# Two half turns moved among the matmuls of the same slice, and a pair of slices of b loaded in two parts

## The chip, the cores and the metric

One core of a Trainium2 chip. The metric is the device time of one launch in microseconds; before the change it is 117.70 us, the median of five runs between 117.55 and 117.79.

## The reference

```
m, k, n, p = 1024, 1024, 2048, 1024        # a: m x k, b: k x n, c: n x p, float32
h = np.matmul(a, b)
h = 0.5 * h * (1 + np.tanh(np.sqrt(2 / np.pi) * (h + 0.044715 * h ** 3)))
return np.matmul(h, c).astype(np.float32)
```

Two matrix products with a gelu between them.

## The kernel before

**Stages.** The first product is made with h transposed: TensorE holds 128 columns of b as weights and streams 512 rows of a, so that 128 x 512 results of h land in one PSUM bank, and ScalarE's gelu writes them to `hT` in bf16. The first 512 columns of b are done with plain bf16 matmuls (`mm1`, line 111). Columns 512 to 1023 (`zero`), columns 1024 to 2047 (`one`) and the whole second product with c (`two`) go through `seven`, a scheme of seven block products in place of eight, with sums and differences of blocks made on VectorE (line 163) and the products on line 205. The change touches the first stage alone.

**Slices and pieces.** The contraction of 1024 is cut into eight slices k of 128. A load of a brings a *piece*: `abq[:, q, h]`, the 512 rows of half h (h = 0 upper, h = 1 lower) by 256 columns, that is slices 2q and 2q + 1. A load of b brings one slice or a pair, 512 columns wide. All but the upper piece 0 of a and the first pair of slices of b are loaded by GpSimd, with a cast from float32 to bf16 on the way, in the order in which they are issued (lines 85 to 101). The first two come through SyncE and are cast on VectorE and ScalarE.

**Turns.** a has to be transposed. `turn(h, q, bank, ab)` does a piece in two halves n = 0, 1, one for each slice: four 128 x 128 transposes on TensorE (line 138) into half n of a PSUM tile, then one copy on VectorE (line 139) into `aT[:, h, 2q + n]`. It is a generator; each `next(tn)` issues one half. From the upper turn of piece 1 on, all turns but the last use bank 7; banks 0 to 3 hold the sums of the upper half and 4 to 6 those of three tiles of the lower half. The fourth lower tile takes bank 7 when the turns there are over, and the last turn takes bank 0 when the gelu has read it.

**Order.** The schedule is written out by hand (`manual_schedule`): each engine runs its instructions in the order of the program. `block(h, tiles, ks)` issues one matmul for each tile and slice. In the loop over q = 1, 2 (lines 244 to 256), k = 2q, four matmuls of the upper half on slice k are followed by the first half of the lower turn of piece q, four on slice k + 1 by its second half; then `zero.t1(4, q)`, one subtraction of 128 x 512 on VectorE, three matmuls of the lower half on slice k, the first half of the upper turn of piece q + 1, three on slice k + 1, and its second half. The last lower turn (lines 262 to 268) lies among matmuls of the fourth lower tile, then come slices 6 and 7 of the lower half (line 274).

Of the kernel before, what the change touches and what calls it, by code (L numbers as in the profile page):

```python
# [19 lines left out]
def kernel(ctx, tc, a, b, c, out):  # L20
    nc = tc.nc
# [3 lines left out]
    H = 512  # L25
# [4 lines left out]
    bv = b.rearrange("(kt p) n -> p kt n", p=128)  # L30
# [9 lines left out]
    def slot(tag, shape, dt, name):  # L40
        return big.tile(shape, dt, name=name, tag=tag)

    def bank(i, shape=(128, H), dt=F32, name="ps"):
        return pp.tile(list(shape), dt, name=name, tag=f"bank{i}", padded_shape=None)
# [14 lines left out]
    b1 = slot("b1", [128, KT, 1024], BF16, "b1")  # L59
# [8 lines left out]
    def a_part(h, q):  # L68
        return av[:, 4 * h:4 * h + 4, ds(q * 256, 256)]

    def b_part(q):
        return bv[:, 2 * q:2 * q + 2, 0:H]
# [6 lines left out]
    def cast_load_a(h, q):  # L79
        nc.gpsimd.dma_start(out=abq[:, q, h], in_=a_part(h, q))  # L80

    def cast_load_b(q):
        nc.gpsimd.dma_start(out=b1[:, 2 * q:2 * q + 2, 0:H], in_=b_part(q))

    cast_load_a(1, 0)
    cast_load_a(0, 1)
    nc.gpsimd.dma_start(out=b1[:, 2, 0:H], in_=bv[:, 2, 0:H])
    cast_load_a(1, 1)
    nc.gpsimd.dma_start(out=b1[:, 3, 0:H], in_=bv[:, 3, 0:H])
    for q in range(2, 4):  # L90
        cast_load_a(0, q)
        cast_load_b(q)
        cast_load_a(1, q)
    for k in range(0, KT, 4):
        nc.gpsimd.dma_start(out=b1[:, k:k + 4, H:], in_=bv[:, k:k + 4, ds(H, H)])
    for n in range(2):
        for k in range(0, KT, 4):
            nc.gpsimd.dma_start(out=b2[:, k:k + 4, ts(n, H)],
                                in_=bv[:, k:k + 4, ds(1024 + n * H, H)])
# [9 lines left out]
    def mm1(p, t, h, ks):  # L109
        for k in ks:  # L110
            nc.tensor.matmul(p, b1[:, k, ts(t, 128)], aT[:, h, k],  # L111
                             start=(k == 0), stop=(k == KT - 1))
# [4 lines left out]
    ps = {(0, t): bank(t) for t in range(4)}  # L117
# [7 lines left out]
    def cast_a(eng):  # L125

        ab = pieces("ab", 2, [128, 4, 256], BF16, "ab")
        copy(eng, ab, sta[:, 0])
        return ab

    def turn(h, q, i, ab):

        banks = i if isinstance(i, tuple) else (i,)
        pts = [bank(x, (128, 2, H), BF16, "pt") for x in banks]
        for n in range(2):
            pt = pts[n % len(pts)]
            for m in range(4):
                nc.tensor.transpose(pt[:, n, ts(m, 128)], ab[:, m, ts(n, 128)], ident)  # L138
            nc.vector.tensor_copy(aT[:, h, 2 * q + n], pt[:, n])  # L139
            yield  # L140
# [8 lines left out]
    def block(h, tiles, ks):  # L149
        for k in ks:  # L150
            for t in tiles:
                mm1(ps[h, t], t, h, (k,))
# [56 lines left out]
    def pair(i):  # L209
        x = slot(f"x{i}", [128, 2, 4, H], F32R, "x1")  # L210
        return x[:, 0], x[:, 1]
# [11 lines left out]
    tn = turn(0, 0, 4, cast_a(nc.vector))  # L223
# [15 lines left out]
    tn = turn(0, 1, 7, abq[:, 1, 0])  # L239
# [3 lines left out]
    zero.t1(4, 0)  # L243
    for q in range(1, 3):
        k = 2 * q
        block(0, range(4), (k,))
        tn = turn(1, q, 7, abq[:, q, 1])
        next(tn)
        block(0, range(4), (k + 1,))
        next(tn)  # L250
        zero.t1(4, q)
        block(1, range(3), (k,))
        tn = turn(0, q + 1, 7, abq[:, q + 1, 0])
        next(tn)
        block(1, range(3), (k + 1,))
        next(tn)
# [6 lines left out]
    mm1(ps[1, 3], 3, 1, range(2))  # L263
    tn = turn(1, 3, 0, abq[:, 3, 1])
    next(tn)
    mm1(ps[1, 3], 3, 1, range(2, 5))
    next(tn)
    mm1(ps[1, 3], 3, 1, (5,))
    zero.t[2], x11 = pair(1)
    zero.t[3], x31 = pair(3)  # L270
    zero.plain_t(2, 0)
# [206 lines left out]
```

## Time and profile before

| | |
|---|---|
| median of five runs | 117.70 us |
| the profiled execution | 117.79 us, span 116.0 us |
| TensorE busy | 110.7 us (95%), 542 matmuls and transposes |
| VectorE busy | 88.8 us (77%) |
| ScalarE busy | 49.5 us (43%) |
| GpSimd busy (issuing loads) | 18.8 us (16%) |
| read from HBM, written | 20.97 MB, 4.19 MB |
| TensorE's granted clock | 1.00 throughout |

The rows that matter lie between 7 and 25 us from the span's start. In a timeline each line has its start, the time from the first start to the last end of the instructions on it, the engine, the line of the kernel, the operation, output and inputs by name, and the count; a bracket at the end tells the idle time of that engine before it and what ended it. Matmuls are pipelined: one shows 0.38 us from start to end, while the next starts sooner, so the pace is read from the starts. PEld is TensorE's load of weights, which runs beside matmuls; PE is the matmul or transpose itself. Copies of a turned half show as `aT<-pt` on VectorE (DVE), transposes as `pt<-ident,abq`.

### The profile page before, as it was taken

How to read it: one execution, taken by the hardware profiler on the slowest of the kernel's cores; microseconds unless marked ns; L12 is line 12 of the kernel's file. 1: busy time of each engine (PE TensorE's matmuls, PEld its weight loads, DVE VectorE, ACT ScalarE, POOL GpSimd, SP SyncE). 2: the span in 40 equal slices, each digit the busy share in tenths (PEclk: the TensorE clock that was granted, in tenths of full speed). 3: DMA queues.
4: the chain of work that ended last, by engine and by line, in shares of the span. 5: the costliest groups of instructions: out<-in, count | busy, mean ns of one | idle time of the engine just before them, and what ended most of it. 6: DMA issues, size and time to landing. Idle time of an engine off the chain costs nothing.

```text
span 116.0 us, 1454 instructions
## 1 busy us (share of the span) xinstructions
PE 110.7 (95%) x542; PEld 77.1 (66%) x542; DVE 88.8 (77%) x104; ACT 49.5 (43%) x82; POOL 18.8 (16%) x31
## 2 busy tenths in 40 slices
PE   7869999999999999999999999999999999999980
PEld 6546555546777447888885444588888888888860
DVE  0334747779999999734699999999999986954670
ACT  5030000899268998166698429600124982000000
POOL 7966754223322000000000000000000000000000
PEclk9999999999999999999999999999999999999999
DMA  2999999999999999998000000070000002014993
GB/s 89 269 197 196 200 201 205 203 206 207 205 210 211 211 212 210 210 213 151 7 0 0 6 0 0 23 248 0 0 0 0 0 2 94 0 75 149 370 371 120
DMA packets 13846, 15.29 MB, mean 132 GB/s; under 512 B 784, under 2 KB 10256, under 8 KB 13840
## 3 DMA queue, kind: packets, MB, share of 16 engines
q0 software_dynamic: 9872, 9.96, 51.5%
q1 hardware_dynamic: 3968, 5.24, 13.0%
q8 instruction: 4, 0.07, 0.2%
q14 instruction: 2, 0.02, 0.0%
HBM read 20.97 MB, written 4.19 MB: 217 GB/s over the span
## 4 chain that ended last, share of the span: by engine, by line
PE 91%; DMA 5%; DVE 1%; SPq 0%; issue 0%
PE ps L205 76%; PE ps L111 12%; DMA stb<-in_b_dram 5%; PE pt L138 3%; DVE b L107 0%; DVE ot L365 0%; SPq L74 0%
## 5 line engine op out<-in xcount | busy, mean ns | idle before, releaser
L205 PE MATMUL ps<-x,s 128*128 128x512 f32 x128 | 29.6, 391 | 0.0
L205 PEld LDWEIGHTS ps<-x,s 128*128 128x128 f32 x128 | 24.0, 188 | 5.1
L205 PE MATMUL ps<-x,x 128*128 128x512 f32 x96 | 22.9, 394 | 0.0
L205 PEld LDWEIGHTS ps<-x,x 128*128 128x128 f32 x96 | 18.0, 188 | 3.9
L111 PE MATMUL ps<-aT,b 128*128 128x512 bf16 x64 | 16.1, 379 | 0.9 <-DVE b L107 0.9
L288 ACT ACTIVATE v<-ps 128x512 f32<-128x512 f32 x10 | 6.0, 599 | 19.5 <-PE ps L205 19.5
L205 PE MATMUL ps<-c_sb,hT 128*128 128x512 bf16 (+1 forms) x72 | 14.2, 356 | 0.0
L205 PE MATMUL ps<-x 128*128 128x512 f32 x56 | 13.2, 393 | 0.0
L115 ACT ACTIVATE hT<-ps 128x512 bf16<-128x512 f32 x14 | 7.3, 595 | 12.9 <-PE ps L111 12.9
L205 PEld LDWEIGHTS ps<-x 128*128 128x128 f32 x56 | 10.2, 188 | 2.7 <-ACT u L288 0.4
L139 DVE COPY aT<-pt 128x512 bf16<-128x512 bf16 x16 | 6.7, 422 | 6.8 <-PE pt L138 6.8
L205 PEld LDWEIGHTS <-hT 128*128 128x128 bf16 x72 | 6.9, 98 | 7.0 <-issue 0.5
L115 ACT ACTIVATE hT<-ot 128x512 bf16<-128x512 f32 x18 | 10.4, 625 | 1.9 <-DVE ot L293 1.8
L205 PE MATMUL ps<-aT,b 128*128 128x512 bf16 x48 | 10.7, 379 | 0.0
L293 DVE TENSOR_TENSOR ot<-ps,u 128x512 f32<-128x512 f32 x10 | 6.7, 688 | 5.2 <-ACT u L288 5.2
L293 DVE TENSOR_TENSOR ot<-ps,v 128x512 f32<-128x512 f32 x10 | 6.7, 687 | 4.9 <-DMA out_dram<-ot 4.0
L163 DVE TENSOR_TENSOR x<-c_sb 128x1024 fp32r<-128x1024 bf16 x8 | 9.2, 1216 | 0.0
L111 PEld LDWEIGHTS <-b 128*128 128x128 bf16 x64 | 5.7, 98 | 5.2 <-DVE b L107 1.0
L205 PEld LDWEIGHTS <-b 128*128 128x128 bf16 x48 | 4.6, 98 | 5.7 <-issue 0.3
L101 POOL DMA_DIRECT2D c_sb<-in_c_dram x8 | 5.6, 704 | 13.0 <-DMA b<-in_b_dram 12.4
L163 DVE TENSOR_TENSOR x<-b 128x1024 fp32r<-128x1024 bf16 (+1 forms) x4 | 7.0, 1751 | 0.8 <-DMA b<-in_b_dram 0.8
L288 ACT ACTIVATE u<-ps 128x512 f32<-128x512 f32 x10 | 5.9, 598 | 3.3 <-PE ps L205 3.2
(43 smaller groups left out, 109.1 us busy)
## 6 DMA issues: line engine op xcount, KB each, us to landing
c_sb<-in_c_dram POOLq DMA_DIRECT2D x8, 512.0 KB, 19.8
b<-in_b_dram POOLq DMA_DIRECT2D x6, 512.0 KB, 15.3
out_dram<-ot SPq DMA_DIRECT2D x10, 256.0 KB, 2.1
abq<-in_a_dram POOLq DMA_DIRECT2D x7, 256.0 KB, 8.5
out_dram<-ot SPq DMA_DIRECT2D x12, 128.0 KB, 2.1
sta<-in_a_dram SPq DMA_DIRECT2D x1, 512.0 KB, 3.4
stb<-in_b_dram SPq DMA_DIRECT2D x1, 512.0 KB, 5.5
b<-in_b_dram POOLq DMA_DIRECT2D x2, 256.0 KB, 9.0
```

The source lines that it names most:

```text
L101: nc.gpsimd.dma_start(out=c_sb[:, t:t + 2], in_=cv[:, t:t + 2])
L111: nc.tensor.matmul(p, b1[:, k, ts(t, 128)], aT[:, h, k], start=(k == 0), stop=(k == KT - 1))
L115: nc.scalar.activation(hT[h][:, t], p, AF.Gelu_apprx_tanh)
L138: nc.tensor.transpose(pt[:, n, ts(m, 128)], ab[:, m, ts(n, 128)], ident)
L139: nc.vector.tensor_copy(aT[:, h, 2 * q + n], pt[:, n])
L163: nc.vector.tensor_tensor(out=dst[:, r], in0=x[:, r], in1=y[:, r], op=op)
L205: nc.tensor.matmul(p[:, ds(c0, w)], l[:, k, ts(j, 128)], r[:, k, ds(c0, w)], start=(start and k == 0), stop=(k == self.kt - 1), skip_group ...
L288: nc.scalar.activation(st, p, AF.Copy)
L293: nc.vector.tensor_tensor(out=ot, in0=p, in1=st, op=ADD)
```

## The change

Loads: the pair of slices 4 and 5 of b is loaded slice by slice, with the lower piece 2 of a between the two. Piece 1 and its slices 2 and 3 keep their order, and the pair of slices 6 and 7 stays one load.

Turns: for q = 1 both halves of the lower turn come among the four upper matmuls of slice 2, the first half after two of them, the second after all four; the four of slice 3 follow together. For q = 2 the first half comes after three matmuls of slice 4, the second after the fourth of slice 4 and three of slice 5. In the last lower turn four matmuls, in place of three, lie between the halves, and the one that came after the second half is gone from there.

```
-    def cast_load_b(q):
-        nc.gpsimd.dma_start(out=b1[:, 2 * q:2 * q + 2, 0:H], in_=b_part(q))
+    def cast_load_b(k, n=1):
+        nc.gpsimd.dma_start(out=b1[:, k:k + n, 0:H], in_=bv[:, k:k + n, 0:H])
 
     cast_load_a(1, 0)
-    cast_load_a(0, 1)
-    nc.gpsimd.dma_start(out=b1[:, 2, 0:H], in_=bv[:, 2, 0:H])
-    cast_load_a(1, 1)
-    nc.gpsimd.dma_start(out=b1[:, 3, 0:H], in_=bv[:, 3, 0:H])
-    for q in range(2, 4):
+    for q in range(1, 3):
         cast_load_a(0, q)
-        cast_load_b(q)
+        cast_load_b(2 * q)
         cast_load_a(1, q)
+        cast_load_b(2 * q + 1)
+    cast_load_a(0, 3)
+    cast_load_b(6, 2)
+    cast_load_a(1, 3)
...
     for q in range(1, 3):
         k = 2 * q
-        block(0, range(4), (k,))
+        ahead = q + 1
+        block(0, range(ahead), (k,))
         tn = turn(1, q, 7, abq[:, q, 1])
         next(tn)
-        block(0, range(4), (k + 1,))
-        next(tn)
+        block(0, range(ahead, 4), (k,))
+        if q == 1:
+            next(tn)
+            block(0, range(4), (k + 1,))
+        else:
+            block(0, range(3), (k + 1,))
+            next(tn)
+            block(0, (3,), (k + 1,))
         zero.t1(4, q)
...
     tn = turn(1, 3, 0, abq[:, 3, 1])
     next(tn)
-    mm1(ps[1, 3], 3, 1, range(2, 5))
-    next(tn)
-    mm1(ps[1, 3], 3, 1, (5,))
+    mm1(ps[1, 3], 3, 1, range(2, 6))
+    next(tn)
```

## The prediction

> **What bounds the kernel now.** I read the page's chain shares first, then the chain in order of time, then the timeline of the stretch that the diff touches, then the waits and the loads.
>
> ```profile
> PE 91%; DMA 5%; DVE 1%; SPq 0%; issue 0%
> ...
> L139 DVE COPY aT<-pt 128x512 bf16<-128x512 bf16 x16 | 6.7, 422 | 6.8 <-PE pt L138 6.8
> ```
>
> TensorE ends the chain in 91% of the span. A copy of a turned half (line 139) takes 422 ns on VectorE, which waits for TensorE in all. The chain in order of time shows how the change's stretch joins the rest:
>
> ```profile
> 13.43 0.22 PE pt L138 x4
> 13.65 0.65 PE ps L111 x3
> 14.29 0.25 PE pt L138 x4
> 14.55 0.65 PE ps L111 x3
> 15.19 0.28 PE pt L138 x4
> ...
> 19.48 2.16 PE ps L111 x10
> ...
> 24.71 88.02 PE ps L205 x400
> ```
>
> Ten matmuls take 2.16 us, so one takes 0.216. Four transposes take 0.22, but at 14.29 they take 0.25 and at 15.19 0.28: something small is waited for there. From 24.71 on TensorE runs 400 matmuls with no other engine in the chain, so a time lost before 24.71 reaches the end whole, and none is given back. What is waited for shows in the timeline (start, us, what; the last bracket is idle time):
>
> ```profile
> 10.19 0.39 PE L138 MATMUL pt<-ident,abq 128*128 128x128 bf16 x4
> ...
> 10.61 0.42 DVE L139 COPY aT<-pt 128x512 bf16<-128x512 bf16 x1 [0.79 <-PE pt L138]
> ...
> 11.09 0.38 PE L138 MATMUL pt<-ident,abq 128*128 128x128 bf16 x4
> ...
> 11.51 0.42 DVE L139 COPY aT<-pt 128x512 bf16<-128x512 bf16 x1 [0.47 <-PE pt L138]
> ...
> 11.85 0.68 DVE L163 TENSOR_TENSOR x<-aT 128x512 fp32r<-128x512 bf16 x1
> ...
> 13.69 0.42 DVE L139 COPY aT<-pt 128x512 bf16<-128x512 bf16 x1 [0.66 <-PE pt L138]
> ...
> 14.03 0.68 DVE L163 TENSOR_TENSOR x<-aT 128x512 fp32r<-128x512 bf16 x1
> 14.16 0.38 PE L138 MATMUL pt<-ident,abq 128*128 128x128 bf16 x4
> ...
> 14.63 0.42 DVE L139 COPY aT<-pt 128x512 bf16<-128x512 bf16 x1
> ...
> 15.10 0.38 PE L138 MATMUL pt<-ident,abq 128*128 128x128 bf16 x4
> ```
>
> Bank 7 is one buffer for all these turns. A half turn starts at 10.19, its copy starts 0.42 later, runs to 11.03, and the second half of the same turn starts at 11.09. At 14.16 a new turn starts 0.05 after the copy of the turn before it ended (13.69 + 0.42 = 14.11). At 14.63 the copy came 0.05 late behind a subtraction of line 163, and the next half came late with it: 15.10 is 0.05 after 14.63 + 0.42. So each half turn waits until the copy of the half before it has ended, inside one turn too, and the starts of two half turns lie at least **0.90 us** apart, or 0.94 with a subtraction before the copy. TensorE's own work between two starts is 0.22 + 0.216 for each matmul between them: 0.65 with two, 0.87 with three, 1.08 with four. Four cover the round trip, three fall 0.03 short, two fall 0.25 short.
>
> **The change part by part.** No engine computes more or less; transposes move among matmuls, and one load becomes two.
>
> *The order on TensorE.* I count the spaces between half turns, from the second half of the upper turn of a's second piece (11.09) to the first matmul of slice 7 behind the last half turn, matmuls between before and after the change in brackets. Upper turn to the first lower half of piece 1 (4, now 2): 1.08 becomes 0.90. First to second lower half (4, now 2): 1.08 becomes 0.94, since the copy is due at 11.99 + 0.42 = 12.41 and the subtraction that started at 11.85 lets a copy start 0.60 later, as from 14.03 to 14.63, at 12.45. On to the next upper turn (3, now 4 + 3 = 7): 0.90 becomes 0.22 + 7 x 0.216 = 1.73. Between its halves (3, 3): 0.94 becomes 0.90, because the subtraction now ends long before. On to the lower turn of piece 2 (4, now 3): 1.08 becomes 0.90. Between its halves (4, 4): 1.08 stays. On to the upper turn of piece 3 (3, now 4): 0.90 becomes 1.08. Between its halves (3, 3): 0.93 (18.17 to 19.10) becomes 0.90. The ten matmuls after it stay. Between the halves of the last lower turn (3, now 4): 0.90 becomes 1.08. From its second half to the first matmul that reads its copy (4, now 3): 1.08 becomes 0.90, since that matmul too needs the copy.
>
> Before: 1.08 + 1.08 + 0.90 + 0.94 + 1.08 + 1.08 + 0.90 + 0.93 + 0.90 + 1.08 = 9.97. After: 0.90 + 0.94 + 1.73 + 0.90 + 0.90 + 1.08 + 1.08 + 0.90 + 1.08 + 0.90 = 10.41. The difference is **+0.44 us**. As waits: two new ones of 0.25 and 0.29 at piece 1; the waits of 3, 7, 3, 6 and 3 hundredths of before become four of about 3.
>
> The second of these waits is the doubtful one, as no row of before has two matmuls there. By the rows at 11.09 and 15.10 it is 0.29. The lower bound is no wait inside a turn: then the same count, with waits only from turn to turn, gives +0.09. The upper bound is a copy that waits for the whole subtraction, 11.85 + 0.68 = 12.53 in place of 12.45: +0.52. I take +0.44, because three half turns inside a turn (11.09, 15.10, 19.10) each start 0.05 to 0.06 after the copy ended. The Trainium skill bears on it: PSUM — Partial Sum Buffer, in its section on bank collisions, says that accesses of two engines to PSUM must be kept apart by bank, not by address. By that rule the halves of one bank wait, as the rows show; by addresses alone the sum would be the +0.09.
>
> Queued behind the waiting transposes are the matmuls of slices 2 and 3, on which only VectorE's later copies and subtractions depend, in the same order as now. Next late is ScalarE's gelu of the first four tiles (20.60, now about 21.04); the first bank it frees is wanted at 21.48, now 21.92, so the distance stays. VectorE is idle 0.76 before 26.25, where a load of b's next columns ends the wait, which covers the 0.44; without that cover it would still cost nothing until the first product with this sum, at 28.0 (27.81 + 0.19, the first of these matmuls having 0.58 in place of 0.39).
>
> *The loads.* GpSimd issues one load more, 0.74 us (the row at 4.29), and the order behind a's upper piece 2 becomes slice 4, a's lower piece 2, slice 5, in place of both slices, then a.
>
> ```profile
> 6.43 0.80 POOL L80 DMA_DIRECT2D abq<-in_a_dram  x1
> 8.38 0.75 POOL L80 DMA_DIRECT2D abq<-in_a_dram  x1 [1.15 <-DMA abq<-in_a_dram]
> ```
>
> ```profile
> 16.12 0.27 PEld L138 LDWEIGHTS <-abq 128*128 128x128 bf16 x4 [0.27 <-DMA abq<-in_a_dram]
> ```
>
> The lower piece 2, issued at 6.43, took 9.6 us and landed at 16.03; its weight load waited for it, the transposes at 16.18 did not lose time (15.32 + 4 x 0.216 = 16.18). So nothing is to be gained there in this execution. From issue and landing: slice 3 at 12.1, upper piece 2 at 13.5, slices 4 and 5 at 14.75, in order of issue, 0.63 us for 128 KB and 1.24 to 1.42 for 256 KB. New landings: slice 4 at 14.1 (wanted at 15.78), the piece at 15.4 (wanted at 16.46), slice 5 at 16.05 (wanted at 16.90). From the ninth load on, GpSimd's issue waits for the landing eight loads back (8.38 after 1.42 + 6.7 = 8.1), so the loads behind are issued one landing later, at most 1.4 us, yet 7 us before their data come; they move at a steady 200 to 211 GB/s. Cost: nothing, hidden by the queue; bound 0 to 0.1 us a landing (two halves at 0.63 to 0.68 against 1.24), with 0.5 us of room at every user. Without the cover, slice 5 would hold TensorE up by what it is late beyond 0.85. SyncE's queue is not passed by anything. A rule that speaks against the split is in DMA: Bandwidth & Descriptors, section on the anatomy of a DMA on the gpsimd path: about 2.0 us fixed for each transfer. If these lay in a row, a's upper piece 3 would land at 19.4 in place of 17.4, 0.8 after it is wanted (18.63), and the sum would be +1.2; the rows at 0.63 us a landing show them overlapped.
>
> **The sum.** The profiled execution took 117.79 us with a span of 116.0, 1.79 around it; it is 0.09 above the median 117.70. It becomes 118.23 with a span of 116.44, and the median 118.14, which I round to 118.15. A measurement of this kernel can tell 0.2% (0.24 us) from no change.
>
> **Rivals.**
> *Waits by turn only.* The second half writes other addresses than the copy reads, so it need not wait: +0.09, 117.8, within 0.2%. Against it stand 15.10 and 19.10. Chance 0.07.
> *The late piece cured.* In the profiled execution a's lower piece 2 arrived with 0.06 us to spare (16.12 against 16.18). If in most executions it comes later, the old order stalls and the new one, landing it 0.65 earlier, does not. It decides from 0.44 us of lateness on: with 0.7, 117.70 + 0.44 - 0.70 = 117.44, faster. For it: the missing spare. Against it: the profiled time, without that stall, is above the median. Chance 0.05.
> *Slice 5 held back.* Were slice 5 to land with the next piece of a, at 17.4, TensorE would wait 0.5 at 16.90: 118.65. For it: a new load in the queue; against it: landings in order of issue. Chance 0.04.
> *Nothing moves as said*: the diff's order is written out by hand and the scheduler follows the program, as the timeline follows the source now. No chance given.
>
> **How the numbers follow.** The forecast has 0.84: 118.15, itself between 117.9 and 118.4 (its bounds +0.2 to +0.52 with 0.1 to 0.15 of spread of the five runs). The range takes that with a little of the rivals: 117.85 to 118.42. Slower: 0.84, less 0.02 for a small outcome, plus 0.04: 0.86. Within 0.2%: 0.07 plus 0.02 plus a little of the cure: 0.10. Faster: 0.04.
>
> **What would show it.** Right: transposes at about 11.99 and 12.93 with idle time of 0.25 and 0.28 before them, released by line 139; the next upper turn at 14.66 in place of 14.16; line 205's chain from about 25.15, still some 88.0 long. The weight load of lower piece 2 no longer waits for a load. Wrong: the second of these transposes at 12.65 (no wait inside a turn), a wait on a load at 16.9, or a chain of line 205 shorter than 88.0, which would mean that the lost time is made good.

## The result and the profile after

The changed kernel takes 117.94 us (median of 31 runs, 117.56 to 118.39) beside 117.68 of the kernel before (54 runs): ratio **1.0022**, 95% interval 1.0015 to 1.0029, which is 0.26 us slower. In its profiled execution it took 118.04 us with a span of 116.2.

The chain's shares on the page of the changed kernel:

```profile
PE 89%; DMA 6%; DVE 2%; POOL 0%; issue 0%; POOLq 0%
```

The chain in order of time, changed kernel:

```profile
...
11.36 0.42 DVE aT L139
11.79 0.60 DVE x L163
12.38 0.35 DVE aT L139
...
12.77 0.38 PE pt L138 x4
...
24.98 87.96 PE ps L205 x400
```

Before, every link from 7.36 to 112.72 was TensorE's. Now the chain leaves it for 1.4 us (11.36 to 12.77): it goes through a copy of a half turn, the subtraction that stands behind it on VectorE, and the next copy. The timeline of that place, changed kernel:

```profile
11.16 0.59 PE L111 MATMUL ps<-aT,b 128*128 128x512 bf16 x2
11.36 0.42 DVE L139 COPY aT<-pt 128x512 bf16<-128x512 bf16 x1 [0.47 <-PE pt L138]
11.70 0.68 DVE L163 TENSOR_TENSOR x<-aT 128x512 fp32r<-128x512 bf16 x1
11.81 0.23 PEld L138 LDWEIGHTS <-abq 128*128 128x128 bf16 x4 [0.56 <-DMA abq<-in_a_dram]
11.84 0.38 PE L138 MATMUL pt<-ident,abq 128*128 128x128 bf16 x4
...
12.06 0.59 PE L111 MATMUL ps<-aT,b 128*128 128x512 bf16 x2
...
12.30 0.42 DVE L139 COPY aT<-pt 128x512 bf16<-128x512 bf16 x1
12.77 0.38 PE L138 MATMUL pt<-ident,abq 128*128 128x128 bf16 x4
```

Two matmuls from 11.16 would end their turn at 11.59, and the transposes start at 11.84, 0.06 after the copy's end (11.36 + 0.42 = 11.78): 0.25 lost. Two more from 12.06 would end at 12.49, the transposes start at 12.77, 0.05 after 12.30 + 0.42: 0.28 lost. These are the two forecast waits, at the forecast's size. For the first of them this execution alone leaves a rival: the load of a's lower piece 1 landed at 11.77, and the weight load at 11.81 waited for it as well. In e2_turn1 and e12_after below that piece landed at 11.32 and 11.45, at least 0.5 before the same half turn (11.85 and 11.96), and the half turn again starts 0.90 after the one before it; so the wait is for the bank. (A modelled end lies later than the pace allows, so idle time of TensorE doesn't show in brackets here.) From the second half of the upper turn of piece 1 to the first matmul on slice 7 of the lower half, the starts in the trace lie 12.80 us apart, in the profile of the kernel before 12.37: **+0.43**, where the forecast had 0.44. Yet the time rose by 0.26 only. The stage itself started 0.15 earlier in this execution (10.94 against 11.09, the second half of the upper turn of piece 1), and that raised the question of the experiments: is the missing 0.18 chance, or something that the kernel before loses?

### The profile page after: what moved, and what is told of

It reads as the page before. It is cut to its first block, busy times and chain, and to the rows that moved or that the text cites. A ratio compares the mean times of both kernels' runs of the same rounds, so it can differ in the third digit from the quotient of the medians.

```text
span 116.2 us, 1454 instructions
## 1 busy us (share of the span) xinstructions
PE 111.4 (96%) x542; PEld 77.3 (67%) x542; DVE 88.8 (76%) x104; ACT 49.5 (43%) x82; POOL 19.3 (17%) x32
## 4 chain that ended last, share of the span: by engine, by line
PE 89%; DMA 6%; DVE 2%; POOL 0%; issue 0%; POOLq 0%
PE ps L205 76%; PE ps L111 10%; DMA abq<-in_a_dram 6%; PE pt L138 3%; DVE aT L139 1%; DVE x L163 1%; DVE ot L371 0%; POOL ident masks.py:199 0%; POOL ident masks.py:197 0%; POOLq masks.py:199 0%; POOLq L468 0%
```

## The experiments

Each is compared with runs of the kernel before on the same chip. The ratios are those recorded with the runs; with twelve runs of a variant the two medians can lie up to about 0.15 us further apart or closer than the ratio says, and where that matters both are given. Theory A: the old order waits for loads in executions other than the one profiled, and the change does away with that. Theory B: the loads bring nothing.

**One part at a time.** *e1_loads* is the kernel before with only the new loads:

```
-    cast_load_a(0, 1)
-    nc.gpsimd.dma_start(out=b1[:, 2, 0:H], in_=bv[:, 2, 0:H])
-    cast_load_a(1, 1)
-    nc.gpsimd.dma_start(out=b1[:, 3, 0:H], in_=bv[:, 3, 0:H])
-    for q in range(2, 4):
+    for q in range(1, 3):
         cast_load_a(0, q)
-        cast_load_b(q)
+        cast_load_b(2 * q)
         cast_load_a(1, q)
+        cast_load_b(2 * q + 1)
+    cast_load_a(0, 3)
+    cast_load_b(6, 2)
+    cast_load_a(1, 3)
```

> The kernel before with the new order of loads alone: slice 4, a's lower piece 2, slice 5. Theory A (the old order of loads makes TensorE wait for a's lower piece 2 in most executions, though not in the one profiled, by about 0.18 us = the forecast's 0.44 less the measured 0.26): 0.1 to 0.2 us faster than before, ratio 0.9983 to 0.9992. Theory B (the missing 0.18 lies elsewhere, the loads cost and bring nothing): 1.0000 within 0.0005. Theory C (an added load makes the loads behind it late): slower by 0.1 us or more.

Measured: 117.67 us, ratio 0.9992 (0.9984 to 1.0001), which is 0.09 us faster, by the medians 0.01. It lies at the edge of theory A and does not exclude B; C is out. Its profile showed a new wait, at the weight load of the last lower turn:

```profile
21.41 0.23 PEld L138 LDWEIGHTS <-abq 128*128 128x128 bf16 x4 [0.48 <-DMA abq<-in_a_dram]
```

That piece landed at 21.37, and TensorE's transposes came 0.15 late. Before, it had landed at 20.06.

*e2_turn1* is the kernel before with only the lower turn of piece 1 moved (the lines of the change's `q == 1` case):

> The kernel before with the lower turn of piece 1 alone moved among the matmuls of slice 2; loads as before. By the count of waits the stretch from the upper turn of piece 1 to the end of the stage grows by 0.47 us less 0.04. Theory A: TensorE comes to a's lower piece 2 0.46 us later, which covers what it waits for that load now, so only 0.2 to 0.3 us slower, ratio 1.0018 to 1.0027. Theory B: 0.40 to 0.47 us slower, 1.0034 to 1.0040.

Measured: 118.04 us, ratio 1.0023 (1.0009 to 1.0037): 0.27 slower, where A expected 0.2 to 0.3 and B 0.40 to 0.47. By the medians it is 0.36, and the upper end of the interval (0.44) touches B, so this run does not decide between them. The waits themselves are there at their size: in its profile the two halves start 0.25 and 0.28 late. So this move alone makes as large a slowdown as the whole change.

*e3_no_q1* is the changed kernel with that move taken back:

```
-        block(0, range(ahead), (k,))
-        tn = turn(1, q, 7, abq[:, q, 1])
-        next(tn)
-        block(0, range(ahead, 4), (k,))
         if q == 1:
+            block(0, range(4), (k,))
+            tn = turn(1, q, 7, abq[:, q, 1])
             next(tn)
             block(0, range(4), (k + 1,))
+            next(tn)
...
```

> The changed kernel with the lower turn of piece 1 back where it was (slices 2 and 3, four matmuls each); the new order of loads and the other two moves stay. Theory A: 0.15 to 0.25 us faster than before, 117.45, ratio 0.998 to 0.9987. Theory B: 0.0 to 0.05 us faster, 0.9996 to 1.0000.

Measured: 117.66 us, ratio 0.9995 (0.9984 to 1.0005). As in e1_loads, the last piece of a landed late, at 21.32, and 0.19 was lost before the last lower turn, so what the loads may bring was spent there. It decided nothing between A and B; it confirms that without the move of piece 1 the slowdown is gone.

*e4_before*, the kernel before once more:

> The kernel before once more, for a second profile of it. Theory A: the weight load of a's lower piece 2 waits for its load, and the transposes start more than 0.02 us after the four matmuls before them end. Theory B: the transposes start with the end of those matmuls, and the start of the stage differs from one profile to the next by 0.1 us or more.

Measured: 117.73 us. The lower piece 2 was not waited for, and the stage started at 11.05 (second half of the upper turn of piece 1). By itself this spoke for B, though the difference of starts that B expected, 0.1 or more, did not show either (11.05 against 11.09).

**Room at the last turn.** *e5_tail* is e1_loads with the first half of the last turn one matmul later:

```
-    mm1(ps[1, 3], 3, 1, range(2))
+    mm1(ps[1, 3], 3, 1, range(3))
...
-    mm1(ps[1, 3], 3, 1, range(2, 5))
-    next(tn)
-    mm1(ps[1, 3], 3, 1, (5,))
+    mm1(ps[1, 3], 3, 1, range(3, 6))
+    next(tn)
```

> The kernel before with the new order of loads (as in e1_loads) and the last lower turn one matmul of the fourth lower tile later: three matmuls, first half, three, second half. In the profile of e1_loads the last piece of a landed at 21.37 in place of 20.06 and TensorE waited 0.15 for it, which may have hidden what the loads bring. Theory A2 (the new order of loads does away with a wait for a's lower piece 2 that the kernel before has in the executions where TensorE starts early): 0.15 to 0.25 us faster than before, ratio 0.9979 to 0.9987, and no wait over 0.03 at the last lower turn. Theory B (the loads bring nothing): 1.0000 within 0.0005.

Measured: 117.82 us, ratio 1.0003 (0.9990 to 1.0015): a miss for A2, and within what B expected. *e6_q2_tail* has the lower turn of piece 2 moved as well:

> As e5_tail, and with the changed kernel's lower turn of piece 2 (three matmuls of slice 4, four to the second half, four behind it). Its waits in the stage are about 0.06 fewer than in e5_tail. Theory A2: 0.2 to 0.3 us faster than before, ratio 0.9975 to 0.9983. Theory B: 0.06 faster, 0.9995.

Measured: 117.56 us, ratio 0.9995 (0.9983 to 1.0006): a miss too, and just B's value. By times alone no version with the new loads was clearly faster so far. But the profiles of both showed a second wait that I had not had in mind. e6_q2_tail, weight loads:

```profile
12.06 0.55 PEld L111 LDWEIGHTS <-b 128*128 128x128 bf16 x4 [0.22 <-DMA b<-in_b_dram]
```

Slice 3 of b landed at 12.02, and the four matmuls on it, due at 11.85, began at 12.06: 0.21 lost. In e5_tail 0.09 were lost at the same place. The new order of loads leaves slice 3 where it was, so neither kernel could be cured of this one. The changed kernel is: its move of piece 1 puts the matmuls on slice 3 some 0.75 us later.

**More executions of the kernel before.** *e7_before* and *e8_before*:

> The kernel before, for a further profile. Theory A2: the upper turn of piece 1 starts its second half anywhere from 10.8 to 11.1 us, and where it starts before 11.0 the transposes of lower piece 2 start later than 5.09 after it, held by the load, so that they never start before 16.03. Theory B: always 5.09 after it.

> The kernel before, for a further profile. Theories as for e7_before.

e7_before took 117.64 us, e8_before 118.01. The matmuls before the transposes of a's lower piece 2, the weight load and the transposes in e7_before:

```profile
14.95 1.03 PE L111 MATMUL ps<-aT,b 128*128 128x512 bf16 x4
...
15.92 0.23 PEld L138 LDWEIGHTS <-abq 128*128 128x128 bf16 x4 [0.44 <-DMA abq<-in_a_dram]
15.92 0.40 PE L138 MATMUL pt<-ident,abq 128*128 128x128 bf16 x4
```

The bracket is idle time of the weight loader, of which most lies beside running matmuls. The four matmuls from 14.95 end their turn at 15.81, and the transposes start at 15.92: TensorE lost 0.11, and 0.05 more at slice 3. In e8_before the weight load waits in the same way until 16.40, and the transposes, due at 16.34, start at 16.41: 0.07 lost. So both waits do happen in the unchanged kernel, as A2 says. The bound that I had set (never before 16.03) fell: it is the landing that holds, and that moves too, to 15.88 in e7_before. The starts fell outside the expected 10.8 to 11.1 as well (10.67 and 11.25). And in e8_before the stage started late (11.25) and still waited, since the loads were later by more.

What the old order would wait for can be worked out for every execution that loads slice 3. With s the start of the second half of the upper turn of piece 1, slice 3 is wanted at s + 1.31 and a's lower piece 2 at s + 5.09; a load is usable 0.04 to 0.05 after it landed. Where the loads stand in the new order, slice 5 lands where the piece did in the old one. The landings are the last of the sixteen completions that the trace has for each load (16.07 for the piece where the prediction, from a rounded duration, had 16.03).

| execution | s | slice 3 landed | piece landed (old place) | lost in the old order |
|---|---|---|---|---|
| before, as shown | 11.09 | 12.11 | 16.07 | 0 |
| e4_before | 11.05 | 12.03 | 15.99 | 0 |
| e7_before | 10.67 | 11.97 | 15.88 | 0.17 |
| e8_before | 11.25 | 12.40 | 16.36 | 0.07 |
| e1_loads | 10.88 | 11.94 | 15.92 | 0 |
| e2_turn1 | 10.95 | 11.97 | 15.92 | 0 |
| e3_no_q1 | 10.83 | 11.98 | 15.96 | 0.08 |
| e5_tail | 11.46 | 12.81 | 16.78 | 0.28 |
| e6_q2_tail | 10.55 | 12.02 | 15.99 | 0.41 |
| changed kernel | 10.94 | 12.41 | 16.39 | 0.41 |
| e11_three | 10.96 | 12.11 | 16.10 | 0.10 |
| e12_after | 11.06 | 12.10 | 16.08 | 0 |

The mean is 0.13 us. It is a calculation on executions of several kernels that are alike up to s; with twelve of them it is rough. The new loads alone do away with the piece's share of it, 0.08 (ratio 0.9993), and that value lies inside the intervals of e1_loads, e3_no_q1, e5_tail and e6_q2_tail, as does 1: these runs could not tell the theories apart.

**The wait taken away from both kernels.** *e9_before_no3* and *e10_after_no3* leave out the load of slice 3, so that the loads behind come sooner (in e9's profile a's lower piece 2 landed at 15.56 and was wanted at 16.16):

```
-    nc.gpsimd.dma_start(out=b1[:, 3, 0:H], in_=bv[:, 3, 0:H])
...
     cast_b(1, nc.scalar)
+    copy(nc.scalar, b1[:, 3, 0:H], b1[:, 2, 0:H])
```

> The kernel before without the load of slice 3 of b; slice 3 is a copy of slice 2, made by ScalarE, so the output is not the reference's. All loads behind land about 0.65 us earlier, so that TensorE can wait neither for slice 3 nor for a's lower piece 2. Theory A2 (in a good part of the executions the kernel before waits for these two, by what the ten profiles so far give 0.14 us on the mean): 0.10 to 0.20 us faster than before, ratio 0.9983 to 0.9992. Theory B (no such waits; the forecast's count of waits was too high for the usual execution): 1.0000 within 0.0005.

> The changed kernel without the load of slice 3, as in e9_before_no3. Theory A2: nothing waits for these loads in the changed kernel, so the time stays at that of the changed kernel, ratio 1.0018 to 1.0026 to before, and 0.40 to 0.45 us above e9_before_no3, which is the count of bank waits alone. Theory B: also as the changed kernel, but 0.26 us above e9_before_no3.

Measured: e9_before_no3 117.42 us, ratio **0.9975** (0.9962 to 0.9988), that is 0.29 faster (0.14 to 0.45; by the medians 0.24); e10_after_no3 117.98 us, ratio **1.0030** (1.0016 to 1.0043). B is out by the first of these: the kernel before gains when its loads come earlier. The changed one doesn't, but that says less, since its loads cost it something new. The two lie 0.56 apart by the medians, 0.65 by the ratios, more than A2's 0.40 to 0.45. Part of that is a wait that my expectation excluded. e10_after_no3, timeline, where line 139 is that of the transposes:

```profile
10.52 0.38 PE L139 MATMUL pt<-ident,abq 128*128 128x128 bf16 x4
...
11.81 0.40 PE L139 MATMUL pt<-ident,abq 128*128 128x128 bf16 x4 [0.48 <-DMA abq<-in_a_dram]
```

This execution started early (10.52); bank 7 was free for the next half turn at 10.52 + 0.90 = 11.42, but a's lower piece 1 let it start at 11.81. The changed kernel wants that piece 0.18 sooner than the kernel before (0.90 against 1.08 after s), so it can give back some of what it saves, in early executions. In the twelve of the table it would not: the piece was usable at least 0.02 before that, so the loss is seen in e10_after_no3 alone.

**A version with neither short space.** *e11_three* has the new loads, the last turn of e5_tail, and the lower turns of both pieces moved by one matmul only (the lines of these turns, against the kernel before):

```
-        block(0, range(4), (k,))
+        block(0, range(3), (k,))
         tn = turn(1, q, 7, abq[:, q, 1])
         next(tn)
-        block(0, range(4), (k + 1,))
+        block(0, (3,), (k,))
+        block(0, range(3), (k + 1,))
         next(tn)
+        block(0, (3,), (k + 1,))
```

> The new order of loads, and the lower turns of pieces 1 and 2 both with three matmuls, first half, four, second half, four; the last lower turn as in e5_tail. By the count of spaces the waits for bank 7 and bank 0 come to about 0.15 us in place of 0.25 (0.66 less the loads' in the changed kernel), slice 3 is wanted 0.03 later than before. Theory A2: 0.1 to 0.25 us faster than before, ratio 0.9979 to 0.9992. Theory B: 0.1 us faster.

Measured: 117.51 us beside 117.66, ratio 0.9985 (0.9970 to 1.0000): the fastest version here that computes all, 0.15 below the kernel before, but with an interval that ends at 1, and both theories allow it. In its profile no space of the moved turns has a wait above 0.04 us.

*e12_after*, the changed kernel beside these:

> The changed kernel once more beside these, for its time on the same chip and a second profile. Theories A2 and B: 1.0015 to 1.0029; in the profile waits of 0.25 and 0.28 us before the two halves of the lower turn of piece 1, and none for slice 3 or a's lower piece 2.

Measured: 118.09 us, ratio 1.0025 (1.0012 to 1.0038), which is 0.29 us, by the medians 0.43. Its halves start 0.90 and 0.93 apart, as forecast: 11.06, 11.96, 12.89.

## Why the prediction was right, and where it was off

**What bounds the kernel: right.** What is lost before 24.7 reaches the end. Line 205's stretch is 87.96 us long against 88.02. Taken by the letter that is shorter than 88.0, the prediction's sign that lost time is made good; but 0.06 is no more than executions of the kernel before differ by (87.99 in e8_before, 88.10 in e7_before). The times say the same. Time less s is 106.70, 106.68 and 106.68 in the three profiled executions that waited for none of these loads (before as shown 117.79 - 11.09, e4_before 117.73 - 11.05, e9_before_no3 117.75 - 11.07), and 107.10 in both of the changed kernel (118.04 - 10.94, 118.16 - 11.06). Against executions without such waits the change costs 0.41 of its 0.43.

**The order on TensorE: right, term by term.** The starts forecast for the moved half turns, 11.99, 12.93 and the next upper turn at 14.66, came at 11.84, 12.77 and 14.50, each about 0.15 earlier, as the whole stage was; measured from s they are 0.90, 1.83 and 3.56 against 0.90, 1.84 and 3.57. The sum over the stage is 0.43 for 0.44.

**The doubtful wait inside a turn: settled.** The second half waited for the copy of the first, behind a subtraction, at 0.28 against 0.29 forecast. The rule of the Trainium skill (PSUM — Partial Sum Buffer, in its section on bank collisions) to keep accesses apart by bank and not by address agrees with this case. The rival "waits by turn only" is out, by the row at 12.77. Its price was wrong: the 0.09 sets the changed kernel without waits inside a turn against the measured 9.97 of before, which has 0.16 of them. Left out on both sides (9.81 and 10.06) the sum is +0.25, so the measured 0.26 alone would not have spoken against this rival; the trace does, with 0.43 in the stage.

**The loads: the mis-sized term.** I wrote that nothing was to be gained there "in this execution", and put the rival of the late piece, on its own from 0.44 us of lateness, at 0.05. The sentence held for the execution that I had, and that was one with no wait for either load. In seven of the other eleven executions of the table the old order would lose between 0.07 and 0.41. What the prediction should have carried is a term of about -0.13 us for the mean of these waits: 0.43 - 0.13 = 0.30, against 0.26 measured (0.18 to 0.34). I saw the piece's 0.06 us to spare and did not turn it into a price; and slice 3, landed at 12.1 and wanted at 12.40, I listed with its landing alone. Of the 0.13, 0.05 fall to slice 3 and 0.08 to the piece (the table's values split by place). The move that costs 0.25 + 0.28 also covers both: it wants slice 3 later by 0.75 and the piece, by the old loads in e2_turn1, by 0.46. So part of its price had been paid already in other executions, as waits for loads. The times of the profiled executions show that as well: time less s, 106.7 without waits, is 106.76 in e8_before, which lost 0.07, and 106.97 in e7_before, which lost 0.16 there and 0.11 further on. How often that happens, and with it the 0.13, is known from the table alone.

**The split of a load: right that it costs nothing at its users,** e1_loads is not slower. The other price, by the Trainium skill (DMA: Bandwidth & Descriptors, in its section on the anatomy of a DMA on the gpsimd path: about 2.0 us fixed for a transfer, which by the prediction's estimate would make +1.2 if they lay in a row), is not borne out: in the changed kernel slices 4 and 5 land at 14.40 and 16.39 with the piece between them at 15.74, 0.64 to 0.65 for a slice. That slice 5 is held back to the next piece (17.74) is out as well. One thing is not settled: a's last piece came late, at a loss of 0.15 and 0.19, in two of the seven executions of the table with the new loads (e1_loads, e3_no_q1) and in none of the five with the old ones. Whether the new order has to do with it was not tried; the changed kernel's own two profiles do not have it.

**Where the line fell.** The measured 117.94 lies in the range and near its lower end; the forecast of 118.15 was 0.21 too high, of which the missing term is 0.13 by the table. That the time still fell inside is in part luck: the range had no place for waits that the change takes away. The direction is sure, but that the slowdown passes 0.2% is not, as the interval begins at 1.0015.

**What stays open.** e9_before_no3 gained 0.29 (0.14 to 0.45), more than the 0.13 of the table. Earlier loads can also help further on: in e7_before a load of b's next columns held up the first product of line 205 on VectorE's results, which starts 3.38 after the line's first in place of 3.27, 0.11 lost. But that is so in none of the other profiles, so on the mean it is little. Either the twelve executions have fewer waits than is usual, or the kernel without that load starts the stage earlier; neither was tried.

## What to carry to other kernels

A half turn through one bank has a round trip (here transposes, copy, transposes: 0.90 us), and the matmuls put between two of them have to cover it; two matmuls more or less decide whether moving work earlier saves anything. A profile is one execution: where a load lands close to the time it is wanted (here 0.06 and 0.29 us before it, with starts that spread over 0.9), price the wait over the spread of starts and landings, not at the nought of the one at hand. When a move costs less than its waits add up to, look for a wait of the old order that it covered.

## What was not expected of the hardware

**The start differs from one execution to the next.** Up to s TensorE, VectorE and ScalarE run the same program in all twelve executions of the table, on the same first loads, yet s lay between 10.55 and 11.46 us from the span's start. b's first slices, on SyncE's queue, landed between 6.38 and 7.40, a's lower piece 0, on GpSimd's, between 7.96 and 8.83, and not always together: the changed kernel's profiled execution had the first at 6.38, the earliest, and the second at 8.44, later than most.

**One of a load's sixteen parts can come far behind the rest.** In e1_loads fifteen parts of a's last piece had completed by 19.87 and the last at 21.37; in e3_no_q1 by 19.91 and at 21.32. In the other ten executions of the table the last part of this load came 0.0 to 0.6 behind the one before it. Loads of b's next columns, twice as large, have a late last part in every profile: that of the first one came at 23.32 in the kernel before as shown, 0.75 behind, and 0.2 to 1.0 behind in the other eleven. What holds these parts up was not tried.
